# Whole float32 instead of split float32 in the last layer's embedding gate

## The chip, the cores and the metric

The kernel runs on one core of one Trainium2 chip. The metric is the device time of one execution in microseconds; a kernel's time is the median of its runs. TensorE multiplies, VectorE (DVE in the profile), ScalarE (ACT) and GpSimd (POOL) work on elements, and SyncE's queue (SP) issues nearly all transfers.

## What is computed

A decoder trunk of two layers over 256 tokens of width 1024. Each layer ends with a feed-forward part, a LayerNorm, and a gate that lets in a per-layer embedding, followed by another LayerNorm. The second layer's feed-forward part is a mixture of eight experts.

```python
for i in range(DEPTH):                       # DEPTH = 2
    h = hybrid_mixer(x, ...)                 # attention, convolution, state space
    x = layer_norm(ALPHA * x + h, ln_g[i, 0], ln_b[i, 0])
    f = swiglu(x, ...) if i % 2 == 0 else moe_swiglu(x, ...)
    x = layer_norm(ALPHA * x + f, ln_g[i, 1], ln_b[i, 1])
    e = (p[i] @ ple_proj[i]) * sigmoid(x @ ple_gate_w[i] + ple_gate_b[i])
    x = layer_norm(ALPHA * x + e, ln_g[i, 2], ln_b[i, 2])
```

Here `p[i]` is 256 x 256, `ple_proj[i]` 256 x 1024 and `ple_gate_w[i]` 1024 x 1024. The change touches the line with `e`, for the second layer alone.

## The kernel before

Tokens stand in two tiles of 128. Weights come in loads of 1 MB (a tile of 128 x 2048 float32, `wraw`) that SyncE's queue issues in order; the tiles for them come in turn from a ring of buffers of several pools (`room`, `turned`). The experts' weights are multiplied as they land, in float32 as they are (lines 1468 and 1503).

Other products are made in three parts. A float32 matrix is split into a high part that is rounded to fp32r and a low part, the rest (`split`, lines 312 to 314: a ScalarE copy, then a subtraction on VectorE or GpSimd). `mm3` (lines 308 to 310) then makes three products, high by high, low by high and high by low, into the same sum in PSUM.

The end of the second layer runs like this:

1. The last expert's output (`mo`, line 1503) is split into `ot` and scattered to the tokens (`sc`, lines 1523 and 1524). VectorE adds the result to `x` (line 1526), first for one tile of tokens and, after that tile's LayerNorm, for the other.
2. LayerNorm of each tile (lines 522 to 532): statistics, root, then two VectorE operations on each half of the row (531, 532). As each half is done, four transposes on TensorE (`xtr`, line 334) bring it into the layout that a product needs, and the transposed x is split into `xh` and `xl` (`make_xT`).
3. `ple_late` loads the embedding `pT` (256 KB) and `ple_proj` (1 MB), splits both with GpSimd making the low parts (`whl`), and makes the products `pp`: 2 tiles of tokens x 2 halves of 512 columns x 2 steps of the sum, each an `mm3`. ScalarE copies them out (line 1120).
4. `ple_load` loads the gate's weights, four loads of 1 MB. `square_parts` splits them, eight rows of 128 x 1024, one per step k of the sum: ScalarE makes `whi`, then two halves of `glo` on GpSimd (k in `POOLW` = 0, 2, 4, 6) or on VectorE (the others), line 553. From k = `GK[1]` = 2 on they are ordered behind the first tile's LayerNorm on the engines.
5. `ple_gate` makes x times the gate's weights (`pg`): for the first tile of tokens in two pieces of 512 columns, for the second in pieces of 512, 256 and 256, each with eight steps k, each step an `mm3`, and a bias product (line 565) ahead of each piece. The second tile's products stand behind the first's on TensorE.
6. `fill` applies tanh, multiplies with `pp` and adds x (lines 1159 to 1161); the last LayerNorm follows, and four stores write the output.

The order of the instructions on an engine isn't the order of the program alone: a scheduler with its own picture of when things are ready sets it, earlier lines of the program first. The ring has 18 buffers while the last two experts are loaded. At the last scatter `turned((self.cp, "xl"))` takes one of them, `xl`, out for the low part of the transposed x; `ple_late` takes out `pp`.

Of the kernel before, what the change touches and what calls it, by code (L numbers as in the profile page):

```python
# [7 lines left out]
F32 = mybir.dt.float32  # L8
F32R = mybir.dt.float32r
I32 = mybir.dt.int32  # L10
U32 = mybir.dt.uint32
AF = mybir.ActivationFunctionType
# [3 lines left out]
P = 128  # L16
D = 1024
S = 256
TT = S // P
KT = D // P  # L20
# [149 lines left out]
RH = 7  # L170
PJ = 8
KL = 4
GK = (9, 2)


GT = ("tr", "tr", "one", "one")
# [16 lines left out]
class Trunk:  # L193
# [122 lines left out]
    def split_scaled(self, hi, lo, t, f):  # L316
# [2 lines left out]
        self.nc.vector.scalar_tensor_tensor(lo, t, f, hi.bitcast(F32), op0=ALU.mult, op1=ALU.subtract)  # L319
        return [(hi[:, i], lo[:, i]) for i in range(2)]  # L320

    def new_xT(self, dt=F32R):

        self.xh, self.xl = (self.cp.tile([P, KT, S], dt, tag=n, name=n) for n in ("xh", "xl"))

    def make_xT(self, src, tt, h):

        nc = self.nc
        ts = slice(tt * P, (tt + 1) * P)
        k4 = slice(4 * h, 4 * h + 4)  # L330
        ps = self.tr("xtr")
        for i in range(4):
            k = 4 * h + i
            self.xtr = nc.tensor.transpose(ps[:, i * P : (i + 1) * P], src[:, k * P : (k + 1) * P], self.ident)
        self.xlast = self.split(self.xh[:, k4, ts], self.xl[:, k4, ts], ps.rearrange("p (k t) -> p k t", k=4))

    def gelu(self, t, u):

# [218 lines left out]
    def square(self, acc, lh, ll, parts, order, bias=None, pieces=HALVES, rows=KT // 2):  # L557


        first = order[:rows]  # L560
        seq = [(k, c) for k in first for c in pieces] + [(k, c) for c in pieces for k in order[rows:]]
        for k, c in seq:
            wh, wl = parts[k]
            if bias is not None and k == order[0]:
                self.nc.tensor.matmul(at(acc, c), self.onesr[0:BK], bias[0:BK, c], start=True, stop=False)
            end = self.mm3(at(acc, c), lh(k), ll(k), wh[:, c], wl[:, c], k == order[0] and bias is None, k == order[-1])
        return end


# [534 lines left out]
    def ple_late(self, l):  # L1104

        a = self.a
        n = 2 * S
        self.ring, self.nload = self.turned((self.xp, "pp")), 0
        self.pp = self.xp.tile([P, TT, D], F32, tag="pp", name="pp")
        pT = list(self.parts(self.load(a["pT"][l].rearrange("(k p) t -> p k t", p=P), 2, S), 2, S, self.nc.gpsimd))  # L1110
        w = list(self.parts(self.load(a["ple_proj"][l].rearrange("(k p) f -> p k f", p=P), 2, D), 2, D, self.nc.gpsimd))
        yield
        for tt in range(TT):
            ts = slice(tt * P, (tt + 1) * P)
            for h in range(2):
                hs = slice(h * 512, (h + 1) * 512)
                ps = self.bank("one", "pp")
                for (k, ph, pl), (_, wh, wl) in zip(pT, w):
                    self.mm3(ps, ph[:, ts], pl[:, ts], wh[:, hs], wl[:, hs], k == 0, k == 1)
                self.nc.scalar.activation(self.pp[:, tt, hs], ps, AF.Copy, scale=0.5)  # L1120
                yield

# [16 lines left out]
    def ple_gate(self, l, raws, low, normed, bias, lnp):  # L1139

        nc = self.nc
        x = self.x
        sp = self.square_parts(range(KT), lambda k: raws[k // 2][:, k % 2], low)
        for k in range(KT):

            with self.after(*normed) if k >= GK[l] else ExitStack():
                parts = next(sp)
        for tt in range(TT):
            ts = slice(tt * P, (tt + 1) * P)
            pieces = PG[l] if tt else HALVES  # L1150
            acc = [self.bank("one", "pg") for _ in pieces]
            with self.tc.issue_after(end.ins) if tt else ExitStack():
                end = self.square(acc, lambda k: self.xh[:, k, ts], lambda k: self.xl[:, k, ts], parts, range(KT), bias, pieces, RG[l] if tt else KT // 2)

            e = self.pp[:, tt]

            def fill(c):
                g = at(acc, c)
                nc.scalar.activation(g, g, AF.Tanh, scale=0.5)
                nc.vector.scalar_tensor_tensor(e[:, c], g, 1.0, e[:, c], op0=ALU.add, op1=ALU.mult)  # L1160
                nc.vector.scalar_tensor_tensor(e[:, c], x[:, tt, c], ALPHA, e[:, c], op0=ALU.mult, op1=ALU.add)

            def done(h, c):
                if l == DEPTH - 1:
                    nc.sync.dma_start(self.out[0, ts, c], x[:, tt, c])
                elif tt:
                    self.late.append((x[:, tt], tt, h))
                else:
                    self.make_xT(x[:, tt], tt, h)

            self.layer_norm(e, fill, lnp, x[:, tt], done, pieces)
# [64 lines left out]
    def moe(self, l, mp):  # L1236
        nc, a, sm = self.nc, self.a, self.sm
        j = l // 2
        xh, xl = self.xh, self.xl
        ts = lambda tt: slice(tt * P, (tt + 1) * P)  # L1240
# [37 lines left out]
        end, norm = self.last  # L1278
# [29 lines left out]
        ps = self.tr("cnt")  # L1308
# [23 lines left out]
        normed = []  # L1332
# [5 lines left out]
        for e in range(NE):  # L1338
# [23 lines left out]
            if e == NE - 2:  # L1362

                lnp = self.ln_params(l, 1, mp, "tl")
                more = mp.tile([P, 2, D], F32R, tag="th", name="more")
                bias = self.ple_bias(l, mp.tile([P, D], F32, tag="h2", name="gb"), more[:, 0])
        advance(self.ple_late(l))
        raws = list(self.ple_load(l))
        low = [t[:, i] for t in [self.room(F32R, "glo").rearrange("p (a d) -> p a d", a=2) for _ in range(4)] for i in range(2)]
        lnp = self.ln_params(l, 2, mp, "tl")  # L1370
        self.ple_gate(l, raws, lambda k: low[k], normed[0], bias, lnp)

    def expert_loads(self, j, e):

# [43 lines left out]
    def expert(self, mp, loads, n, xe, Dm, D2, comb, y, ahead=None, done=None):  # L1418
# [3 lines left out]
        nc = self.nc  # L1422
# [5 lines left out]
        def pair(name):  # L1428
            acc = self.pair(name)
            if n is not None:  # L1430
                for h in range(2):
                    nc.vector.memset(acc[h][rows[1 - h]], 0.0)  # L1432
            return acc
# [19 lines left out]
        for ci, (c0, cw) in enumerate(CHUNKS):  # L1453
            hw, ku = cw // 2, 2048 // cw
            accs = []
            for wi in range(2):
                acc = pair("mgu")
# [33 lines left out]
        acc = pair("mo")  # L1491
# [22 lines left out]
        def scatter():  # L1514
            normed = ()
            if done:
                self.ring, self.nload = self.turned((self.cp, "xl")), 0
                self.new_xT()
            for tt in range(TT):
                sc = self.pair("sc")  # L1520
                for h in range(2):
                    hs = slice(h * 512, (h + 1) * 512)
                    mm(sc[h], DT[0][:, h, tt], ots[h][:, 0], start=True, stop=False)
                    mm(sc[h], DT[0][:, h, tt], ots[h][:, 1], start=False, stop=True)
                    with self.after(*normed):
                        nc.vector.scalar_tensor_tensor(y[:, tt, hs], sc[h], comb[tt], y[:, tt, hs], op0=ALU.mult, op1=ALU.add)
                if done:
                    normed = done(tt)[1:]

        if n is None or done:  # L1530
            scatter()
        else:
            self.todo.append(scatter)
# [109 lines left out]
def at(acc, c):  # L1643

    return acc[(0, None, 1, 2)[c.start // 256]][:, : c.stop - c.start]
# [45 lines left out]
```

## Time and profile before

| | |
|---|---|
| median of 3 runs | 1606.78 us (1604.98 to 1609.79) |
| the profiled execution | 1610.99 us, of which its span is 1608.8 us |
| granted TensorE clock, mean | 0.959 |
| TensorE busy | 1454.2 us (90% of the span) |
| VectorE busy | 678.0 us (42%) |
| ScalarE busy | 401.3 us (25%) |
| GpSimd busy | 266.0 us (17%) |

Times in the profile count from the start of the span. A busy TensorE is not TensorE at its peak: an instruction's shown duration overlaps that of the next, so the distance between two starts is the better measure of its cost. A whole float32 product shows as two records of the same line, a product of fp32r parts as one. `PEclk` is the share of TensorE's 2.4 GHz that was granted; 0.50 is the level of 1.2 GHz. A line of `--timeline` form gives the start, the duration of the group, engine, line, operation, output <- inputs, and in brackets the idle time before it and what ended that.

### The profile page before, as it was taken

To read this page: it belongs to the slowest core of one execution; us is meant where nothing else is said; L and a number is where in the kernel's file an instruction comes from. 1 tells how busy PE (TensorE), PEld (TensorE's weight loads), DVE (VectorE), ACT (ScalarE), POOL (GpSimd) and SP (SyncE) were. 2 spreads that over 40 slices of the span, in tenths; PEclk is the share of its full clock that TensorE was granted. 3 is DMA by queue.
4 is the path that set the end of the run, shared out by engine and by line. 5 is a ranking of instruction groups with operands and counts; after the bars stand their busy time and mean duration, and the time that the engine had idled before them with its cause. 6 is when DMAs were issued, how large, how long until landed. Compare 5 with 4: busy or idle time off the path is not lost. (4 is left out here: it accounts for less than half of the span.)

```text
span 1608.8 us, 16526 instructions
## 1 busy us (share of the span) xinstructions
PE 1454.2 (90%) x6318; PEld 832.5 (52%) x6319; DVE 678.0 (42%) x1105; ACT 401.3 (25%) x719; POOL 266.0 (17%) x205
## 2 busy tenths in 40 slices
PE   6776999999888699998899999999999998998776
PEld 6544788876675475432344643444644454342234
DVE  8989648646778955222121103121102102122137
ACT  6454555434466431100001001000000000000023
POOL 4855106612124511000000000000000000010012
PEclk9787999999998888999999999999999999999999
DMA  7431365553462049999999999999898878999971
GB/s 250 137 152 40 124 214 187 192 170 131 170 192 111 27 158 401 403 408 405 407 409 402 409 344 389 408 410 400 299 308 272 301 238 281 362 408 409 402 288 53
DMA packets 139625, 445.28 MB, mean 277 GB/s; under 512 B 7408, under 2 KB 19312, under 8 KB 138496
## 3 DMA queue, kind: packets, MB, share of 16 engines
q1 hardware_dynamic: 138496, 437.42, 73.3%
q0 software_dynamic: 1024, 6.38, 1.1%
q8 instruction: 76, 1.25, 0.3%
q14 instruction: 29, 0.24, 0.0%
HBM read 442.72 MB, written 1.05 MB: 276 GB/s over the span
## 5 line engine op out<-in xcount | busy, mean ns | idle before, releaser
L1468 PE MATMUL mgu<-wraw,xe 128*64 128x512 f32 (+3 forms) x2048 | 548.5, 542 | 25.4 <-DMA wraw<-in_moe_w_dram 17.3
L1468 PEld LDWEIGHTS mgu<-wraw,xe 128*64 128x64 f32 (+1 forms) x2048 | 238.3, 157 | 318.4 <-issue 246.9
L1503 PE MATMUL mo<-wraw,ht 128*64 128x512 f32 (+1 forms) x896 | 272.0, 595 | 12.4 <-DMA wraw<-in_moe_w_dram 12.4
L1503 PEld LDWEIGHTS mo<-wraw,ht 128*64 128x64 f32 (+1 forms) x896 | 101.0, 157 | 172.0 <-issue 143.1
L314 DVE TENSOR_TENSOR whl<-wraw,whl 128x1024 fp32r<-128x1024 f32 (+2 forms) x106 | 136.5, 1297 | 81.7 <-ACT whl L313 81.1
L313 ACT ACTIVATE whl<-wraw 128x1024 fp32r<-128x1024 f32 (+3 forms) x109 | 107.5, 994 | 138.3 <-PE fffn_w L310 44.6
L1476 DVE TENSOR_TENSOR hb<-hb,mgu 128x512 f32<-128x512 f32 (+1 forms) x64 | 37.9, 618 | 236.1 <-PE mgu L1468 235.7
L510 POOL DMA_DIRECT2D lnp<-in_lnp_dram x5 | 2.8, 566 | 772.6 <-ACT xe L1397 744.1
L1449 ACT ACTIVATE ht<-hT 128x512 f32<-128x512 f32 (+1 forms) x32 | 17.4, 544 | 393.4 <-PE hT L1444 378.0
L314 DVE TENSOR_TENSOR ot<-mo,ot 128x512 fp32r<-128x512 f32 x16 | 10.6, 688 | 243.1 <-ACT ot L313 243.1
L1432 DVE MEMSET mgu<- 64x512 f32 x128 | 62.1, 485 | 100.2 <-ACT hb L1475 84.1
L1447 DVE COPY ht<-hT 128x512 f32<-128x512 f32 (+1 forms) x32 | 20.0, 625 | 140.7 <-PE hT L1444 136.7
L310 PE MATMUL fffn_w<-whl,xh 128*128 128x512 f32 (+1 forms) x192 | 71.8, 374 | 0.0
L309 PE MATMUL fffn_w<-whl,xl 128*128 128x512 f32 (+1 forms) x192 | 71.7, 373 | 0.0
L308 PE MATMUL fffn_w<-whl,xh 128*128 128x512 f32 (+1 forms) x192 | 71.4, 372 | 0.0
L1475 ACT ACTIVATE hb<-mgu 128x512 f32<-128x512 f32 (+1 forms) x64 | 32.4, 543 | 152.1 <-PE mgu L1468 149.0
L313 ACT ACTIVATE ot<-mo 128x512 fp32r<-128x512 f32 x16 | 9.0, 596 | 239.6 <-PE mo L1503 239.6
L957 DVE SCALAR_TENSOR_TENSOR cy<-upad,pk,cy 128x256 f32<-128x256 f32 x60 | 56.6, 943 | 1.2
L308 PEld LDWEIGHTS fffn_w<-whl,xh 128*128 128x128 f32 x192 | 36.1, 188 | 6.7
L309 PEld LDWEIGHTS fffn_w<-whl,xl 128*128 128x128 f32 x192 | 36.1, 188 | 6.6
L310 PEld LDWEIGHTS fffn_w<-whl,xh 128*128 128x128 f32 x192 | 36.1, 188 | 6.2
L1444 PEld LDWEIGHTS hT<-sqr,hb 128*128 128x128 f32 x224 | 24.8, 140 | 24.7 <-issue 20.4
(371 smaller groups left out, 2147.0 us busy)
## 6 DMA issues: line engine op xcount, KB each, us to landing
wraw<-in_moe_w_dram SPq DMA_DIRECT2D x336, 1024.0 KB, 17.5
wraw<-in_ffn_w_dram SPq DMA_DIRECT2D x33, 1024.0 KB, 5.2
wraw<-in_cmp_w_dram SPq DMA_DIRECT2D x8, 1024.0 KB, 5.6
wraw<-in_w_out_dram SPq DMA_DIRECT2D x8, 1024.0 KB, 7.2
wraw<-in_ple_gate_w_dram SPq DMA_DIRECT2D x8, 1024.0 KB, 5.0
wraw<-in_w_in_dram SPq DMA_DIRECT2D x8, 792.0 KB, 5.9
wraw<-in_w_in_dram SPq DMA_DIRECT2D x8, 768.0 KB, 8.0
lnp<-in_lnp_dram POOLq DMA_DIRECT2D x5, 1024.0 KB, 5.2
```

What stands on the lines that cost most here:

```text
L308: mm(dst, xh, wh, start=start, stop=False)
L309: mm(dst, xl, wh, start=False, stop=False)
L310: return mm(dst, xh, wl, start=False, stop=stop)
L313: h = self.hi = self.nc.scalar.activation(dh, src, AF.Copy)
L314: return h, (low or self.nc.vector).tensor_tensor(dl, src, dh.bitcast(F32), op=ALU.subtract)
L957: nc.vector.scalar_tensor_tensor(y0, u(0, k), w(0, k), y0, op0=ALU.mult, op1=ALU.add)
L1432: nc.vector.memset(acc[h][rows[1 - h]], 0.0)
L1444: nc.tensor.transpose(ps[:, i * P : (i + 1) * P], hbs[h][:, i * P : (i + 1) * P], self.ident)
L1468: mm(dst, x, wk, start=k == 0, stop=k == KT - 1)
L1475: nc.scalar.activation(hb[:, :hw], accs[0][h][:, :hw], AF.Silu)
L1476: nc.vector.tensor_mul(hb[:, :hw], hb[:, :hw], accs[1][h][:, :hw])
L1503: mm(dst, x, w[:, i, h * 512 : (h + 1) * 512], start=k == 0, stop=k == NK - 1)
```

## The change

In the second layer the embedding's products `pp` and the gate's `pg` take their operands as they are, in float32. `ple_late` no longer calls `parts`, and each `mm3` is one `matmul`. `make_xT` copies the transposed x into one float32 tile (`new_whole_xT`) and makes no low part. `ple_gate` is called without `low`: nothing is split, and the condition on `GK[1]` goes with it. The four buffers for `glo` are not taken, and the ring keeps `xl` as a buffer for loads. The first layer stays as it was.

```diff
+    def new_whole_xT(self):
+        self.xh, self.xl = self.cp.tile([P, KT, S], F32, tag="xh", name="xw"), None
@@ make_xT
-        self.xlast = self.split(self.xh[:, k4, ts], self.xl[:, k4, ts], ps.rearrange("p (k t) -> p k t", k=4))
+        v = ps.rearrange("p (k t) -> p k t", k=4)
+        if self.xl is None:
+            self.xlast = [nc.scalar.activation(self.xh[:, k4, ts], v, AF.Copy)]
+        else:
+            self.xlast = self.split(self.xh[:, k4, ts], self.xl[:, k4, ts], v)
@@ square
-            end = self.mm3(at(acc, c), lh(k), ll(k), wh[:, c], wl[:, c], k == order[0] and bias is None, k == order[-1])
+            start, stop = k == order[0] and bias is None, k == order[-1]
+            if len(parts[k]) == 1:
+                end = self.nc.tensor.matmul(at(acc, c), lh(k), parts[k][0][:, c], start=start, stop=stop)
+            else:
+                wh, wl = parts[k]
+                end = self.mm3(at(acc, c), lh(k), ll(k), wh[:, c], wl[:, c], start, stop)
@@ ple_late
-        pT = list(self.parts(self.load(a["pT"][l].rearrange("(k p) t -> p k t", p=P), 2, S), 2, S, self.nc.gpsimd))
-        w = list(self.parts(self.load(a["ple_proj"][l].rearrange("(k p) f -> p k f", p=P), 2, D), 2, D, self.nc.gpsimd))
+        pT = self.load(a["pT"][l].rearrange("(k p) t -> p k t", p=P), 2, S)
+        w = self.load(a["ple_proj"][l].rearrange("(k p) f -> p k f", p=P), 2, D)
...
-                for (k, ph, pl), (_, wh, wl) in zip(pT, w):
-                    self.mm3(ps, ph[:, ts], pl[:, ts], wh[:, hs], wl[:, hs], k == 0, k == 1)
+                for k in range(2):
+                    self.nc.tensor.matmul(ps, pT[:, k, ts], w[:, k, hs], start=(k == 0), stop=(k == 1))
@@ ple_gate
+        if low is None:
+            parts = [(raws[k // 2][:, k % 2],) for k in range(KT)]
@@ moe
-        low = [t[:, i] for t in [self.room(F32R, "glo").rearrange("p (a d) -> p a d", a=2) for _ in range(4)] for i in range(2)]
-        self.ple_gate(l, raws, lambda k: low[k], normed[0], bias, lnp)
+        self.ple_gate(l, raws, None, normed[0], bias, lnp)
@@ expert, scatter()
-                self.ring, self.nload = self.turned((self.cp, "xl")), 0
-                self.new_xT()
+                self.new_whole_xT()
```

## Rows read from the trace of the kernel before

**Rows 1.** Busy time by stretch: engines' busy us (instructions), PEclk, DMA share, GB/s.

```profile
1548.03:1551.33 3.30, 2.38 (x8) 1.34 (x8) 2.59 (x4) 1.09 (x2) 0.71 (x1) 1.00 1.03 410
1551.33:1566.19 14.86, 9.85 (x33) 7.00 (x32) 10.47 (x12) 6.79 (x10) 5.12 (x2) 0.77 0.40 151
1566.19:1587.23 21.04, 14.53 (x60) 9.49 (x59) 19.55 (x21) 11.08 (x14) 12.40 (x9) 1.00 0.14 51
1587.23:1600.29 13.06, 13.02 (x76) 10.80 (x75) 9.94 (x18) 4.39 (x6) 0.00 (x0) 1.00 0.11 40
1600.29:1608.80 8.51, 0.00 (x0) 0.00 (x0) 4.51 (x9) 1.95 (x3) 0.00 (x0) 0.75 0.16 62
```

**Rows 2.** Waits, 1545 to 1609 us: waiter <- releaser, us in total, times, longest.

```profile
PE pg L310 <- DVE glo L553: 4.7, 3, 2.5
...
PE pp L310 <- POOL whl L314: 3.5, 2, 1.8
```

**Rows 3.** Timeline of SyncE's queue, from the embedding's load on.

```profile
1529.84 2.31 SPq L249 DMA_DIRECT2D wraw<-in_pT_dram  x1
1532.24 2.31 SPq L249 DMA_DIRECT2D wraw<-in_ple_gate_w_dram  x1
1534.60 0.46 SPq L249 DMA_DIRECT2D wraw<-in_ple_proj_dram  x1
1535.77 6.94 SPq L249 DMA_DIRECT2D wraw<-in_ple_gate_w_dram  x2
1558.16 0.37 SPq L249 DMA_DIRECT2D wraw<-in_ple_gate_w_dram  x1
```

**Rows 4.** Timeline of ScalarE, VectorE and GpSimd: splits, and two LayerNorms.

```profile
1546.72 0.63 ACT L313 ACTIVATE whl<-wraw 128x512 fp32r<-128x512 f32 x1 [33.16 <-DMA wraw<-in_ple_gate_w_dram]
...
1551.88 2.00 ACT L313 ACTIVATE whl<-wraw 128x1024 fp32r<-128x1024 f32 x2 [2.71 <-issue]
...
1553.01 5.12 POOL L314 TENSOR_TENSOR whl<-wraw,whl 128x1024 fp32r<-128x1024 f32 x2 [4.27 <-ACT whl L313]
...
1553.12 2.79 DVE L531 SCALAR_TENSOR_TENSOR x<-x,mv,lnp 128x512 f32<-128x512 f32 x1
...
1602.34 0.75 DVE L531 SCALAR_TENSOR_TENSOR x<-pp,mv,lnp 128x512 f32<-128x512 f32 x1
...
1603.20 0.75 DVE L532 SCALAR_TENSOR_TENSOR x<-x,rs,lnp 128x512 f32<-128x512 f32 x1
...
1604.65 0.75 DVE L532 SCALAR_TENSOR_TENSOR x<-x,rs,lnp 128x512 f32<-128x512 f32 x1
```

**Rows 5.** Groups by shape on TensorE, the experts' whole float32 products.

```profile
L1468 PE MATMUL mgu<-wraw,xe 128*128 128x512 f32 x576 | 249.8, 593 | 2.0 <-ACT ot L313 0.7 <-ACT hb L1475 0.7 <-DVE mgu L1432 0.6
...
L1468 PE MATMUL mgu<-wraw,xe 128*128 128x256 f32 x192 | 42.4, 379 | 0.0
```

**Rows 6.** Timeline of TensorE: first products of successive `mm3`, 512 and 256 columns.

```profile
1588.48 0.40 PE L308 MATMUL pg<-whi,xh 128*128 128x512 f32 x1
...
1589.18 0.40 PE L308 MATMUL pg<-whi,xh 128*128 128x512 f32 x1
...
1594.24 0.28 PE L308 MATMUL pg<-whi,xh 128*128 128x256 f32 x1
...
1594.60 0.28 PE L308 MATMUL pg<-whi,xh 128*128 128x256 f32 x1
```

**Rows 7.** Timeline of TensorE and ScalarE: transposes, their copy, the bias products.

```profile
1564.73 0.60 PE L334 MATMUL xtr<-sqr,x 128*128 128x128 f32 x4
...
1565.37 0.60 ACT L313 ACTIVATE xh<-xtr 128x512 fp32r<-128x512 f32 x1 [0.31 <-PE xtr L334]
...
1566.19 0.73 PE L565 MATMUL pg<-more,sqr 33*128 33x512 f32 x2
```

**Rows 8.** Busy time by stretch of 1 us, columns as in Rows 1.

```profile
1557.00:1558.00 1.00, 0.00 (x0) 0.00 (x0) 1.00 (x1) 0.00 (x0) 1.00 (x1) 0.50 0.00 0
...
1563.00:1564.00 1.00, 1.00 (x6) 0.95 (x5) 0.00 (x0) 0.29 (x1) 0.00 (x0) 0.67 0.00 0
```

More of the change, by code (lines that the diff above doesn't have):

```diff
@@ L172 @@
 KL = 4
-GK = (9, 2)
+GK = (9,)
 GT = ("tr", "tr", "one", "one")
@@ L562, in square @@
         for k, c in seq:
-            wh, wl = parts[k]
             if bias is not None and k == order[0]:
                 self.nc.tensor.matmul(at(acc, c), self.onesr[0:BK], bias[0:BK, c], start=True, stop=False)
-            end = self.mm3(at(acc, c), lh(k), ll(k), wh[:, c], wl[:, c], k == order[0] and bias is None, k == order[-1])
+            start, stop = k == order[0] and bias is None, k == order[-1]
[4 more added lines that the diff above has]
+                end = self.mm3(at(acc, c), lh(k), ll(k), wh[:, c], wl[:, c], start, stop)
         return end
@@ L1142, in ple_gate @@
         x = self.x
[L1143 to L1147, printed above, removed]
+        if low is None:
+            parts = [(raws[k // 2][:, k % 2],) for k in range(KT)]
+        else:
+            sp = self.square_parts(range(KT), lambda k: raws[k // 2][:, k % 2], low)
+            for k in range(KT):
+                with self.after(*normed) if k >= GK[l] else ExitStack():
+                    parts = next(sp)
         for tt in range(TT):
```

## The prediction

> **What bounds the kernel now.** The change touches only what follows the last expert, so I read the busy time by stretch for the end of the span first. After the scatter's products (they end at 1551.33) come 35.9 us in which TensorE is busy for 24.4 us, then the second tile's gate, 13.06 us without a gap, then 8.51 us of tail without TensorE [rows 1]. The tail hangs on the last product alone. So the time is set by when TensorE can end its queue, and the stretch from 1551.33 to 1587.23 is where it waits. The view of waits says for what: 4.7 us for VectorE's low parts of the gate's weights, 3.5 us for GpSimd's low parts of the embedding [rows 2].
>
> Two more things stand in that stretch. The first: the fourth load of the gate, issued at 1558.16, right as GpSimd's second `whl` ends (1553.01 + 5.12 = 1558.13); the other loads were out by 1542.71 [rows 3, 4]. That one was held by a buffer that the splitting occupied. The second: TensorE's clock fell to 1.2 GHz, the granted clock being 0.50 by 1557 and back in the slice from 1563 [rows 8], after TensorE had had little to do while it waited for splits.
>
> **The change, part by part.**
>
> *TensorE pays more per product.* A whole float32 product of 512 columns costs two records of 249.8/576 = 0.434 us, thus 0.867; one of 256 columns 2 x 42.4/192 = 0.442 [rows 5]. An `mm3` takes 1589.18 - 1588.48 = 0.70 us at 512 columns and 0.36 at 256 [rows 6]. The counts: `pp` has 8, the gate's first tile 16, the second tile 8 of 512 and 16 of 256. At full clock that is 8 x 0.70 + 16 x 0.70 + (8 x 0.70 + 16 x 0.36) = 28.2 us before and 6.9 + 13.9 + 14.0 = 34.8 after. So TensorE's own work grows by 6.6 us.
>
> The Trainium skill speaks more strongly against the change: "FP8 and Floating Point Precision", section TensorE Precision Notes, gives true FP32 as four passes through the array. Against the split's three, each at the price of these rows, that would be 4/3 of 28.2 = 37.6 us, an estimate that would take 2.8 us off the gain below; the experts' rows (0.867 against 4/3 of 0.70 = 0.93) differ from that by 7%, and I go by the rows.
>
> *The splits go.* Nothing stands between a load and its product any more: three `whl` on ScalarE and GpSimd, eight `whi` and sixteen halves of `glo`. Loads alone are left. The experts' last load has landed by about 1546.1, since the embedding's 256 KB are there at 1546.72 [rows 4] and at 410 GB/s [rows 1] 1 MB (1.049 million bytes) takes 2.56 us, 256 KB 0.64. Without the splitting buffers, all six loads can go out in a row in the program's order: `ple_proj` is there at about 1549.3, the gate's four at 1551.9, 1554.4, 1557.0 and 1559.5. In the kernel before, `ple_proj` stood behind one gate load, hence its arrival just before 1551.88 [rows 3, 4]. Both ends are before or close to the end of the scatter, so `pp` can fill the time in which LayerNorm runs.
>
> *LayerNorm of x speeds up.* Line 531 took 2.79 us at 1553.12 while GpSimd was splitting `whl`, and 0.75 in the last LayerNorm, where GpSimd is idle [rows 1, 4]. With the subtractions gone I take the last one's pace: from the start of 531 to the end of its first half's 532 is 1603.95 - 1602.34 = 1.61 us, to the end of the second half 3.06. From 1553.12 that gives halves of x at 1554.7 and 1556.2. Four transposes take 0.60, their ScalarE copy 0.60 [rows 7]; so the first tile's transposed x is there by about 1557.5, while TensorE still has `pp` to do. The second tile's chain has the same form (two additions more) and should be ready near 1562, a dozen microseconds before TensorE asks for it; VectorE's `xl` and `glo` no longer stand in its queue.
>
> *New queue of TensorE, at full clock.* From 1551.33: `pp` 6.9, transposes of the first tile 2 x 0.60 = 1.2, the gate's first tile 0.73 for bias [rows 7] + 13.9, transposes of the second 1.2: the second tile starts at 1575.3 instead of 1587.23. Its stretch took 13.06, of which the splits are 8 x 0.70 + 16 x 0.36 = 11.4; the other 1.7 (bias, changes of operands) stays: 14.0 + 1.7 = 15.7, end at 1591.0. Then the tail of 8.51: 1599.5, against 1608.8. So -9.3 us. From this I give back one ScalarE copy of 0.60, which TensorE may have to sit out if `pp` ends before the transposed x is copied: -8.7. In other words, the waits and the half clock give 15.3 us, TensorE's dearer products take 6.6 of it.
>
> *What I cost at nothing.* The loads after 1551 lie beside `pp` and the first steps k (the last load, for k = 6 and 7, lands at about 1559.5, and the gate's first tile asks for it after 4 steps x 2 pieces, some 7 us into it). If one is late, the price is its lateness. The last LayerNorm's parameters are loaded once line 532 has run for the second tile; that point moves forward with it, by more than the first `fill` does. The ring's extra buffer `xl` takes a load where it was taken out before: nothing waits. ScalarE and VectorE lose work, and the work that hides is all theirs.
>
> *From profile to median.* The profiled execution took 1610.99, 2.2 above its span and 4.2 above the median of 1606.78. The difference is applied to the median: 1606.78 - 8.7 = 1598.1.
>
> **The rivals.**
>
> *A. `pp` stands ahead of the scatter (chance 0.13).* The scheduler takes what it believes is ready. On ScalarE it put the split of the embedding ahead of the expert's `ot`, and ScalarE stood idle for 33.16 us on it [rows 4]; harmless there. If TensorE's queue gets `pp` ahead of `sc`, the scatter waits until 1549.3 + 6.9 = 1556.2, instead of starting around 1548.7: LayerNorm and the first gate products come 7.5 us later less what is already done. The transposed x would be there at 1557.5 + 7.5 = 1565.0, and then 14.6 + 1.2 + 15.7 + 8.5 follow: 1605.0, -3.8 us, that is 1603.0. Against it: the scatter is earlier in the program, and before, all of `sc` ran first.
>
> *B. The clock falls as it did (0.13).* For it: TensorE was at 1.2 GHz for nearly 7 us here [rows 8]. Float32 products at half clock cost double, so 6.8 us at 0.50 cost 3.4: -5.3 us, 1601.5. The Trainium skill, "TensorE: Matmul & The Clock Gate", Part 1, has activity itself release the throttle; the trace agrees in that the clock came back in a slice in which TensorE was busy throughout [rows 8]. Against it: with `pp` following the scatter at once, no stretch like that of 1551 to 1557 is left.
>
> *C. Slower: `pp` stands ahead of the last expert's own products (0.06).* If it comes ahead of the last j pairs of loads of `mo`, TensorE waits for `ple_proj` and does `pp` until 1556.2, and then has those pairs to do before `ot`, each at up to 2 x 2.56 = 5.1 us, the pace of the loads with which TensorE keeps up today. With j = 1 the last expert ends at 1561.3 instead of 1548.0, 13.3 later; the transposed x comes at 1557.5 + 13.3 = 1570.8, and the end is 1570.8 + 40.0 = 1610.8, 2.0 later than now. Each further pair adds 5.1, so from j = 2 it is slower by more than 0.3%: 1615.9 in the profile, 1613.9 as a median. Against it: loads land in order, so when `ple_proj` is there the experts' products are all ready, and come first.
>
> *D. A gate load is still held (0.06).* If the load for k = 0 and 1 went out as late as before, at 1558.16, it would be there at 1563.3 at the latest, taking twice its 2.56 us; the gate's first tile, due at 1559.4, would start 3.9 later: -4.8, 1602.0. Against it: no splitting buffer is left that could hold it.
>
> **How the numbers follow.** My forecast as summed up has 0.62; its own range is 1595 to 1601: below by `pp` filling the gaps of the scatter (0.9 idle of 3.30 [rows 1]) and by the 1.7 of changes shrinking, above by 2 or 3 us of an unlucky order on TensorE; the runs of before scatter by 2 to 3 us each way by themselves. B ends at 1601.5, D at 1602.0, A at 1603.0. The range for 8 in 10 is 1594.5 to 1603.5. A measurement of this kernel can tell about 0.3%, 4.8 us: the border is 1602.0. Faster: the forecast's 0.62, most of B and D, and some of A: 0.82. Same: the rest of A, C with j = 1: 0.13. Slower: 0.05.
>
> **What would show it.** Right: no wait of TensorE for DVE or POOL after the scatter, `pp` in 0.87 us steps from 1551.5 on, line 531 at 0.75 us, no instruction of line 553, six loads in a row, the second tile's gate as long as 15.7 us and starting near 1575, a clock of 1.00 up to the end of the gate, tail 8.5. Wrong: `sc` later than 1549, a granted clock of 0.50 between 1550 and 1590, a step of the gate at more than 0.9 us, or a load of the gate issued after 1545.

## The result

The changed kernel takes 1598.45 us (median of 8 runs, 1595.83 to 1601.54), the kernel before 1609.59 us beside it (8 runs, 1604.98 to 1611.45): a ratio of 0.9937, 95% interval 0.9925 to 0.9948, so 8 to 12 us faster. A second measurement on another occasion gave 0.9938 (0.9925 to 0.995).

The profiled execution has a span of 1595.2 us. Part of its distance to the 1608.8 of before isn't the change's: its scatter ended at 1547.14, that of before at 1551.33 [rows 1], and in two profiles of the changed kernel itself the scatter ended at 1547.14 and 1551.89. What comes ahead of the scatter moves by several microseconds from one execution to the next. So I compare from the end of the scatter to the end of the span, which I call the remainder: 1608.80 - 1551.33 = 57.47 before, 1595.20 - 1547.14 = 48.06 after (48.01 in the second profile). That is -9.4 us, inside the interval of the timed runs.

Busy time by stretch, changed kernel, columns as in [rows 1], with the engines in the order PE, PEld (TensorE's weight loads), DVE, ACT, POOL. The stretches are the scatter; embedding and transposes; gate of the first tile; gate of the second; tail.

```profile
1543.84:1547.14 3.30, 2.38 (x8) 1.53 (x9) 2.59 (x4) 2.37 (x3) 0.00 (x0) 1.00 1.03 412
1547.14:1555.22 8.08, 8.08 (x25) 3.47 (x24) 7.83 (x15) 3.49 (x7) 0.00 (x0) 1.00 0.70 281
1555.22:1571.03 15.81, 15.81 (x44) 7.08 (x43) 3.91 (x7) 3.66 (x5) 0.56 (x1) 1.00 0.19 67
1571.03:1586.60 15.57, 15.47 (x52) 9.44 (x51) 9.31 (x17) 4.39 (x6) 0.00 (x0) 1.00 0.09 34
1586.60:1595.20 8.60, 0.00 (x0) 0.00 (x0) 4.51 (x9) 1.95 (x3) 0.00 (x0) 0.73 0.16 61
```

From 1547.14 to 1586.60 TensorE is busy for all but 0.1 us, at a granted clock of 1.00 (2.4 GHz). The 35.9 us ahead of the second tile [rows 1] are now 23.9, the second tile takes 15.57 instead of 13.06, and the tail is the same within 0.1.

The waits of TensorE, changed kernel, from the scatter on, are only the scatter's own:

```profile
PE sc L1536 <- ACT ot L313: 0.7, 1, 0.7
...
PE sc L1537 <- DVE ot L314: 0.2, 1, 0.2
```

SyncE's queue, changed kernel: all six loads in a row, against [rows 3], where the last stood until 1558.16.

```profile
1525.52 2.31 SPq L249 DMA_DIRECT2D wraw<-in_pT_dram  x1
1527.92 2.31 SPq L249 DMA_DIRECT2D wraw<-in_ple_proj_dram  x1
1530.32 8.88 SPq L249 DMA_DIRECT2D wraw<-in_ple_gate_w_dram  x4
```

TensorE's and VectorE's timeline, changed kernel. The embedding's products start when the scatter ends, each of two records, and make room for the transposes; line 539 is the old 531 and takes 0.75 us where it took 2.79 [rows 4].

```profile
1547.14 3.59 PE L1131 MATMUL pp<-wraw 128*128 128x512 f32 x8
...
1548.94 0.75 DVE L539 SCALAR_TENSOR_TENSOR x<-x,mv,lnp 128x512 f32<-128x512 f32 x1
...
1550.70 0.63 PE L338 MATMUL xtr<-sqr,x 128*128 128x128 f32 x4
...
1552.55 2.74 PE L1131 MATMUL pp<-wraw 128*128 128x512 f32 x6
...
1555.22 0.50 PE L572 MATMUL pg<-more,sqr 33*128 33x512 f32 x1
...
1571.03 0.49 PE L572 MATMUL pg<-more,sqr 33*128 33x512 f32 x1
```

### The profile page after: what moved, and what is told of

Read it like the earlier page. It is cut to its first block, busy times and chain, and to the rows that moved or that the text cites. A ratio compares the mean times of both kernels' runs of the same rounds, so it can differ in the third digit from the quotient of the medians.

```text
span 1595.2 us, 16373 instructions
## 1 busy us (share of the span) xinstructions
PE 1453.8 (91%) x6270; PEld 824.7 (52%) x6271; DVE 657.8 (41%) x1093; ACT 391.1 (25%) x708; POOL 247.6 (16%) x194
## 5 line engine op out<-in xcount | busy, mean ns | idle before, releaser
L313 ACT ACTIVATE whl<-wraw 128x1024 fp32r<-128x1024 f32 (+2 forms) x106 | 104.8, 996 | 104.1 <-PE fffn_w L310 44.6
## 6 DMA issues: line engine op xcount, KB each, us to landing
wraw<-in_ple_gate_w_dram SPq DMA_DIRECT2D x8, 1024.0 KB, 10.7
```

The costliest lines, as they stand in the source:

```text
L313: h = self.hi = self.nc.scalar.activation(dh, src, AF.Copy)
```

## The experiments

Ratios are to the kernel before, timed beside it on the same chip. The remainder runs from the end of the scatter (0.23 us after its last product starts) to the end of the span of one profile, and the last column compares it with the 48.06 of the changed kernel.

| run | ratio (95% interval) | remainder, us | against the change |
|---|---|---|---|
| before | 1 | 57.47 | +9.4 |
| changed, again | 0.9938 (0.9925 to 0.995) | 48.01 | 0.0 |
| embedding whole, gate split | 0.9972 (0.996 to 0.9983) | 51.41 | +3.4 |
| gate whole, embedding split | 0.999 (0.9981 to 0.9999) | 54.96 | +6.9 |
| half the first tile's steps | 0.9903 (0.9888 to 0.9917) | 41.20 | -6.9 |
| embedding behind LayerNorm | 0.9974 (0.9963 to 0.9984) | 54.09 | +6.0 |
| unread parts | 0.9997 (0.9987 to 1.0008) | see below | +7.7 |
| unread parts behind the scatter | 1.0006 (0.9995 to 1.0016) | 58.42 | +10.4 |
| of these, GpSimd's alone | 0.997 (0.9958 to 0.9982) | 53.15 | +5.1 |
| of these, VectorE's alone | 0.9948 (0.9935 to 0.9962) | 48.91 | +0.9 |
| split, but no subtractions | 0.9911 (0.9897 to 0.9924) | 42.84 | -5.2 |
| second tile split again | 0.993 (0.9917 to 0.9943) | 45.47 | -2.6 |

**The two halves of the change.** The embedding alone, in the kernel before:

```diff
-        pT = list(self.parts(self.load(a["pT"][l].rearrange("(k p) t -> p k t", p=P), 2, S), 2, S, self.nc.gpsimd))
+        pT = self.load(a["pT"][l].rearrange("(k p) t -> p k t", p=P), 2, S)
...
-                for (k, ph, pl), (_, wh, wl) in zip(pT, w):
-                    self.mm3(ps, ph[:, ts], pl[:, ts], wh[:, hs], wl[:, hs], k == 0, k == 1)
+                for k in range(2):
+                    self.nc.tensor.matmul(ps, pT[:, k, ts], w[:, k, hs], start=(k == 0), stop=(k == 1))
```

> The kernel before, with the embedding's products alone made in whole float32; the gate stays split. My theory (the gain is TensorE's waits for splits, in two places, less dearer products): pp is 6.9 us without a wait, GpSimd no longer slows line 531 (0.75 instead of 2.79 us) and the clock stays at 1.00, so the gate starts 5 to 6 us earlier, but its first tile still takes about 20 us, waiting for glo on VectorE: -4 to -6 us against before, ratio about 0.997. Rival 1 (all of it is the gate's splits): no change, ratio 1.000. Rival 2 (all of it is the embedding's splits, which delay LayerNorm): about -9 us, 0.994.

-6.1 us in the remainder, at the edge of what was expected (the timed ratio gives -4.5). TensorE's wait for x, and three of VectorE's lines, in this kernel:

```profile
PE xtr L334 <- DVE x L532: 6.8, 3, 3.6
```

```profile
1550.61 1.79 DVE L531 SCALAR_TENSOR_TENSOR x<-x,mv,lnp 128x512 f32<-128x512 f32 x1
...
1552.32 2.38 DVE L553 TENSOR_TENSOR glo<-wraw,whi 128x512 fp32r<-128x512 f32 x2
...
1563.84 1.79 DVE L531 SCALAR_TENSOR_TENSOR x<-x,mv,lnp 128x512 f32<-128x512 f32 x1
```

The wait isn't the expected one: TensorE no longer waits for low parts of the gate at all, but for x out of a LayerNorm whose line 531 takes 1.79 instead of 0.75. Two of VectorE's subtractions for the gate now stand in the first tile's LayerNorm. In the kernel before, VectorE's first one came behind it:

```profile
1568.38 1.74 DVE L553 TENSOR_TENSOR glo<-wraw,whi 128x512 fp32r<-128x512 f32 x1
```

The gate alone, the mirror image (the lines with a minus put back into the changed kernel):

> The changed kernel, with the embedding's products split as before; the gate is whole. My theory: pp waits for whl on GpSimd, LayerNorm of the first tile is as slow as before, the clock falls to 0.50 for some us, the gate starts near 1566 (in times of the kernel before); then its two tiles run without a wait, 14.6 + 1.2 + 15.7 us, and the tail of 8.5: -2 to -4 us against before, ratio about 0.998. Rival 1 (all is the gate's splits): -9 us, 0.994. Rival 2 (all is the embedding's): the dearer products show alone, +4 us, 1.002.

-2.5 us, as expected (-1.6 by the timed ratio). TensorE's wait for the embedding's parts is the one of [rows 2] to the tenth, one gate load is issued late again, and the clock falls as in [rows 8]. Waits of TensorE, SyncE's queue, and one stretch of that kernel:

```profile
PE pp L310 <- POOL whl L314: 3.5, 2, 1.8
```

```profile
1536.06 22.78 SPq L249 DMA_DIRECT2D wraw<-in_ple_gate_w_dram  x3
```

```profile
1557.00:1559.00 2.00, 0.50 (x1) 0.50 (x2) 2.00 (x2) 0.00 (x0) 1.44 (x1) 0.53 0.00 0
```

So neither half is the whole: 6.1 and 2.5 of the 9.4.

**Does TensorE's queue alone set the end now?** Four steps k of the first tile's gate left out:

```diff
-                end = self.square(acc, lambda k: self.xh[:, k, ts], lambda k: self.xl[:, k, ts], parts, range(KT), bias, pieces, RG[l] if tt else KT // 2)
+                end = self.square(acc, lambda k: self.xh[:, k, ts], lambda k: self.xl[:, k, ts], parts, range(KT if tt or l < DEPTH - 1 else KT // 2), bias, pieces, RG[l] if tt else KT // 2)
```

> The changed kernel, with four of the eight steps k of the gate's first tile left out (half of that sum isn't made). It measures whether TensorE's queue alone sets the end now: if so, 8 whole products of 0.867 us fewer make it 6.9 us shorter than the changed kernel, ratio about 0.9895 against before. Rival (a load of the gate, LayerNorm or the fill of the first tile sets the end as well): less than 4 us shorter, 0.991 or more.

The timed ratio lies between the two expectations; the remainder decides. It is 6.9 us shorter, to the tenth what eight whole products cost. TensorE's bias products that open the first and the second tile stand 8.94 us apart instead of 15.81:

```profile
1556.11 0.50 PE L572 MATMUL pg<-more,sqr 33*128 33x512 f32 x1
...
1565.05 0.49 PE L572 MATMUL pg<-more,sqr 33*128 33x512 f32 x1
```

So nothing else is close behind: the second tile's LayerNorm and the fill of the first tile let the end come 6.9 us earlier.

**What covers LayerNorm?** The embedding's products put behind the first tile's transposes:

```diff
...
+                with self.after(self.xtr0):
                     for k in range(2):
                         self.nc.tensor.matmul(ps, pT[:, k, ts], w[:, k, hs], start=(k == 0), stop=(k == 1))
```

> The changed kernel, with the embedding's products ordered on TensorE behind the transposes of the first tile's x, so that nothing covers LayerNorm of that tile. My theory: the products' work (6.9 us) is the cover of that LayerNorm; without it TensorE stands idle from the scatter to the transposes, some 3.6 us plus 0.7, and the end comes about 4 us later than in the changed kernel, more (up to 8) if the clock falls meanwhile: ratio 0.996 to 0.999. Rival: the idle time is made good elsewhere, less than 2 us later.

+6.0 us, within the wider bound. Waits and stretches of this kernel:

```profile
PE xtr L338 <- DVE x L542: 4.2, 2, 3.4
```

```profile
1550.00:1553.00 3.00, 0.27 (x2) 0.00 (x0) 2.86 (x7) 0.29 (x1) 0.00 (x0) 1.00 1.04 414
1553.00:1556.00 3.00, 1.50 (x8) 1.32 (x9) 2.96 (x5) 0.60 (x1) 0.00 (x0) 0.84 0.80 321
1556.00:1559.00 3.00, 3.00 (x7) 1.28 (x6) 2.46 (x5) 0.60 (x1) 0.00 (x0) 0.60 0.09 36
```

(`xtr0` is the last transpose of the first tile.) TensorE stands idle for 4.2 us, then its clock falls: a granted 0.84 and 0.60 over 3 us each are means over both levels, and amount to 0.96 + 2.40 = 3.4 us at 1.2 GHz, worth 1.7 us of work. Together 5.9.

**Waits for parts, or engines that make parts?** The same splits made into buffers that nothing reads, so that no product depends on them:

```diff
+    def unread_parts(self, raws, normed):
...
+        for src, h, o in jobs:
+            self.split(h, o, src, nc.gpsimd)
+        for n in range(KT):
...
+            with self.after(*normed) if n >= 2 else ExitStack():
+                nc.scalar.activation(h, s, AF.Copy)
+                for c in range(0, D, 512):
+                    (nc.gpsimd if n in POOLW else nc.vector).tensor_tensor(o[:, c : c + 512], s[:, c : c + 512], h[:, c : c + 512].bitcast(F32), op=ALU.subtract)
```

(`jobs` are the embedding and both halves of its weights; the loop over n is the gate's.)

> The changed kernel, with all splits of weights made as before on ScalarE, GpSimd and VectorE into buffers of their own that nothing reads; the loads go out as in the changed kernel. My theory has two halves: products that don't wait for parts, and a LayerNorm that nothing slows. If the second half counts, the transposed x comes 3 to 4 us late and TensorE waits for it, and VectorE's glo delays the second tile: 2 to 6 us of the gain are lost, ratio 0.995 to 0.998. Rival (only the products' own dependence on the parts counts, LayerNorm's pace is hidden): as the changed kernel, ratio 0.9935 to 0.994.

By the timed ratio the whole gain is gone, more than the theory had it; in the profile 7.7 us of it. Two of the causes are seen in the waits of TensorE: 3.8 instead of 0.7 us for the last expert's `ot`, because ScalarE had the embedding's split ahead of it, and 2.6 us for x.

```profile
PE sc L1557 <- ACT ot L313: 3.8, 1, 3.8
PE xtr L338 <- DVE x L540: 2.6, 1, 2.6
```

The first is a fault of the experiment: before, those splits didn't delay the scatter. (The 7.7: from the first product of the scatter to the end 55.21 against 50.66, plus the 3.1 by which it came late.) So the run was made again with all splits ordered behind ScalarE's split of `ot`:

```diff
+        behind = self.hi
         for src, h, o in jobs:
+            with self.after(behind):
                 self.split(h, o, src, nc.gpsimd)
...
-            with self.after(*normed) if n >= 2 else ExitStack():
+            with self.after(*normed) if n >= 2 else self.after(behind):
```

> The run with unread parts once more, with all these splits ordered behind ScalarE's split of the last expert's output, so that they can't delay the scatter (in the first version the embedding's split stood ahead of it and cost 3.1 us). My theory: LayerNorm's pace and VectorE's share in the second tile's chain remain, 2 to 4 us later than the changed kernel: ratio 0.995 to 0.997. Rival (the loss of that run was the delayed scatter alone): as the changed kernel plus less than 1 us, ratio 0.994.

+10.4 us: as slow as before, though the scatter isn't delayed and no product waits for a part. Waits of TensorE, VectorE's timeline, and the clock in this kernel:

```profile
PE xtr L338 <- DVE x L540: 7.2, 3, 4.5
```

```profile
1550.71 4.51 DVE L1408 TENSOR_TENSOR dead<-wraw,dead 128x512 fp32r<-128x512 f32 x2
...
1555.32 1.57 DVE L540 SCALAR_TENSOR_TENSOR x<-x,rs,lnp 128x512 f32<-128x512 f32 x1
```

```profile
1557.00:1559.00 2.00, 1.96 (x6) 0.73 (x6) 1.97 (x2) 0.60 (x1) 2.00 (x2) 0.65 0.00 0
1559.00:1561.00 2.00, 1.01 (x5) 0.71 (x5) 2.00 (x3) 0.60 (x1) 0.69 (x1) 0.50 0.00 0
```

Two subtractions of 512 columns took 4.51 us on VectorE while GpSimd was subtracting too, in the middle of the first tile's LayerNorm, where the kernel before had none of VectorE's. TensorE waited 7.2 us for x, and its clock fell, so that the rest of the embedding's products ran mostly at 1.2 GHz (0.50). My estimate of 2 to 4 us had left both out.

To see which engine it is, the same run without VectorE's subtractions (`range(0, D if n in POOLW else 0, 512)`), and without GpSimd's subtractions (`range(0, 0 if n in POOLW else D, 512)` and no GpSimd part of the embedding). ScalarE's copies are made in both:

> The changed kernel with unread parts behind the scatter, but VectorE's halves (k = 1, 3, 5, 7) left out: ScalarE's copies and GpSimd's subtractions alone. In the run with all of them the end came 10.4 us later than in the changed kernel, counted from the scatter. If GpSimd slows VectorE's LayerNorm by itself (line 531 at 2.8 instead of 0.75 us while GpSimd subtracts), TensorE waits 3 us or more for the first tile's x: 3 to 6 us later than the changed kernel, ratio 0.9955 to 0.998. If it doesn't: less than 1 us, 0.9935 to 0.9945.

> The changed kernel with unread parts behind the scatter, but GpSimd's subtractions left out: ScalarE's copies and VectorE's halves for k = 1, 3, 5, 7 alone. If the two engines hinder each other, VectorE's eight halves are short (0.68 us each, 5.4 in all, most of it where TensorE still has work): 0 to 2 us later than the changed kernel, ratio 0.9935 to 0.995. If VectorE's queue by itself is what delays LayerNorm: 3 us or more, 0.9955 or more.

Both sizes came out as the theory had them: +5.1 with GpSimd alone, +0.9 with VectorE alone, and 10.4 with both. Lines of VectorE, TensorE's wait and, for the first, a stretch, with GpSimd's subtractions alone:

```profile
1550.27 0.87 DVE L539 SCALAR_TENSOR_TENSOR x<-x,mv,lnp 128x512 f32<-128x512 f32 x1
...
1552.61 0.17 DVE L535 RECIPROCAL rs<-rs 128x1 f32<-128x1 f32 x1 [1.46 <-ACT rs L534]
...
1553.82 1.77 DVE L539 SCALAR_TENSOR_TENSOR x<-x,mv,lnp 128x512 f32<-128x512 f32 x1
```

```profile
PE xtr L338 <- DVE x L540: 4.5, 4, 1.8
```

```profile
1556.00:1559.00 3.00, 1.68 (x7) 1.07 (x8) 3.00 (x4) 1.40 (x3) 3.00 (x3) 1.00 0.00 0
```

then with VectorE's alone:

```profile
1550.62 1.29 DVE L1408 TENSOR_TENSOR dead<-wraw,dead 128x512 fp32r<-128x512 f32 x2
...
1553.09 0.74 DVE L539 SCALAR_TENSOR_TENSOR x<-x,mv,lnp 128x512 f32<-128x512 f32 x1
```

```profile
PE xtr L338 <- DVE x L540: 0.8, 1, 0.8
```

GpSimd does no work of LayerNorm, and yet beside it VectorE's operations can take more than twice as long; not each does, as the first half's line 539 took 0.87. Not all of the 5.1 us is GpSimd's: VectorE also waits 1.46 us for the root, which ScalarE makes behind its copies. Those copies and VectorE's subtractions together cost 0.9 in the other run, so that at least 4.2 should be GpSimd's. The Trainium skill, "SBUF — State Buffer", section Who interferes with whom, says that a VectorE instruction with two inputs in SBUF contends with a GpSimd instruction that reads SBUF. The trace agrees: lines 539, 540 and the subtractions have two such inputs, and 539 takes 1.77 us beside GpSimd's subtractions and 0.74 without them.

**The other way round: parts without subtractions.** The kernel before, with three products and ScalarE's high parts, where the third product reads the high part again:

```diff
-            self.split(hi, lo, flat, low)
+            if low is None:
+                self.split(hi, lo, flat, low)
+            else:
+                nc.scalar.activation(hi, flat, AF.Copy)
+                lo = hi
```

(and likewise in `square_parts`, for the last layer; the transposed x keeps its low part, which VectorE makes).

> The kernel before, with three products per step and ScalarE's high parts of the weights, but without any subtraction for their low parts: the third product reads the high part once more (the embedding and the gate in the last layer are computed without the weights' low parts). Theory A (what held TensorE back is VectorE and GpSimd, busy with subtractions, and LayerNorm behind them): TensorE has 6.6 us less work than in the changed kernel and waits little, so it is as fast as that or up to 5 us faster, ratio 0.990 to 0.994. Theory B (waiting for parts as such, ScalarE's high parts included, held it back): less than half of the change's gain, ratio 0.997 or more.

Theory A: a remainder 5.2 us shorter than the changed kernel's. Products still depend on parts, eleven ScalarE copies of them, and TensorE waits for one of these only:

```profile
PE pp L312 <- ACT whl L276: 1.5, 1, 1.5
```

The 6.6 us that whole products cost TensorE more, less that wait of 1.5, are 5.1. The run takes away both the subtractions' work and the waiting for their results, so it doesn't tell these two apart.

**A version that beats both?** The second tile's gate in split products, the parts made while TensorE works on the first tile:

```diff
+            if low is None and tt:
+                parts = self.second_parts(raws, parts, ts, behind)
...
+            for k in range(FIRST, KT):
...
+                nc.scalar.activation(hi[:, c], src, AF.Copy)
+                nc.vector.tensor_tensor(lo[:, c], src, hi[:, c].bitcast(F32), op=ALU.subtract)
```

(`FIRST` is 0; the second tile's transposed x is split likewise, and all of it is ordered behind that tile's first LayerNorm.)

> The changed kernel, but the gate's second tile of tokens is made in three split products per step again, with the parts made on ScalarE and VectorE while TensorE makes the first tile (VectorE sat idle for 11.8 us there). My theory: TensorE's queue alone sets the end, so the second tile's products cost 11.4 instead of 14.0 us and the end comes 2 to 2.7 us earlier, ratio about 0.992, against 0.9937 for the changed kernel. Rival: the splits (8 to 9 us of ScalarE, 12 us of VectorE) are late for the second tile or hold up the first tile's fill, and it is no faster than the changed kernel, or up to 3 us slower.

The remainder is 2.6 us shorter than the changed kernel's, by the 2.6 that the products differ. The second tile's first piece takes 1579.99 - 1573.84 = 6.15 us, against 7.48 in the changed kernel, and VectorE has its subtractions done by 1570.9:

```profile
1573.84 0.49 PE L573 MATMUL pg<-more,sqr 33*128 33x512 f32 x1
...
1579.99 0.38 PE L573 MATMUL pg<-more,sqr 33*128 33x256 f32 x1
```

```profile
1567.39 3.49 DVE L1166 TENSOR_TENSOR gl<-wraw,gh 128x1024 fp32r<-128x1024 f32 x3
```

The timed ratios, 0.993 and 0.9938, have overlapping intervals: one profile shows the gain, the timed runs can't tell it. The 0.9938 is the changed kernel's, measured once more for this comparison:

> The changed kernel itself, beside the other three on the same chip: 0.9925 to 0.995 of before, as the base for their differences.

## Why the prediction was right, point by point

The forecast was -8.7 us, 1598.1. Measured were 1598.45, which is -10.1 us by the timed ratio, and -9.4 in the remainder. That the time is met within 0.4 us is in part luck: the forecast started from 1606.78, the median of 3 runs, and the 8 runs beside the changed kernel gave 1609.59. The fairer test is the change itself, and its parts:

- *The price of whole products* held. `pp` and two groups of transposes fill 8.08 us, which is 6.9 + 1.2. The second tile took 15.57 us where 15.7 were reckoned, and from the end of the scatter to its start there were 23.9 us where 24.0 were. The run with half the steps gives 6.86 / 8 = 0.86 per product on the end time itself. The estimate from four passes against three (37.6 us instead of 34.8) isn't borne out: 0.867 is 3.7 times the 0.233 that one product of an `mm3` takes.
- *The 0.60 us for a ScalarE copy* that I gave back weren't needed: six records of `pp` stand behind the second group of transposes and cover it. Without it the sum was -9.3.
- *The cover* held: `pp` stands where LayerNorm runs, and moving it away costs 6.0 us.
- *The loads* went out in a row as reckoned; none was waited for.
- *The rivals* A, B and D (`pp` ahead of the scatter, a fallen clock, a held gate load) did not occur, nor C. The clock did matter for the kernel before, and it fell again in experiments that left TensorE waiting for x: to a mean of 0.60 over 3 us with the embedding moved, to 0.50 with the unread parts.
- *What the waits meant* was read as the profile shows it, but not in full. The prediction took "PE waits for DVE glo" and "POOL whl" as TensorE waiting for parts, and the faster LayerNorm as a smaller effect that `pp` would hide. In the kernel before, the other waits behind the scatter are these:

```profile
PE pp L308 <- ACT whl L313: 1.5, 1, 1.5
PE pg L310 <- POOL glo L553: 1.0, 2, 0.5
PE xtr L334 <- DVE x L532: 0.8, 1, 0.8
```

With [rows 2] that is 10.7 us of waiting for parts and 0.8 for x. The experiments show what lies behind the waits. The parts cost about 16.0 us, the gain of 9.4 and the 6.6 by which whole products are dearer. Without the weights' subtractions, but with ScalarE's high parts, 57.47 - 42.84 = 14.6 of these come back; waiting for ScalarE is the rest. And the subtractions can cost 10.4 of the 16.0 with no product waiting for them, because VectorE and GpSimd are busy and slow each other while LayerNorm needs VectorE. The sum came out right because it took away both the waits and the slow LayerNorm, and needed no division between them.

What stays open: how much of the kernel before's loss was waiting for the low parts and how much was the two engines' hindering each other. The run of +10.4 us doesn't settle it, since it put VectorE's subtractions into the first LayerNorm, where the kernel before had none, and TensorE waited 7.2 us for x in it against 0.8 before. In every run the low parts were made by one of these two engines. Open too is why the part ahead of the scatter differs by 4.7 us between two profiles of one kernel.

## What to carry to other kernels

A trick that saves TensorE time can cost more on the engines that prepare its operands: look at what else these engines have to do in that stretch, and whether the wait that the profile names is for a product or for an engine that is busy with it. Where TensorE is idle anyway, its dearest form may be the fastest; where it is the bound and other engines are idle, the split form may pay again, as one profile of the second tile has it (2.6 us). Give TensorE independent work, as the embedding's products, for the time in which a LayerNorm runs: here its granted clock then stayed at 1.00, and without it fell to a mean of 0.60 over 3 us.

## What the runs showed of the hardware

- GpSimd slows VectorE on two-input operations: 512 columns of line 539 took 0.74 us alone and 0.87 to 1.77 beside GpSimd's subtractions (2.79 in [rows 4]), and two subtractions on VectorE 1.29 alone and 4.51 beside GpSimd's. The cost isn't additive: 0.9 us with VectorE's subtractions, 5.1 with GpSimd's, 10.4 with both.
- A pause of TensorE can be paid twice: with the embedding moved, 4.2 us of waits (the longest 3.4) were followed by 3 us at a mean granted clock of 0.60, and the whole delay was 6.0 us. With GpSimd's subtractions alone, 4.5 us of waits in four pieces (the longest 1.8) left it at 1.00.
